# Rotating 96 images by 90 degrees: the first 2 MB loaded as 16 and 112 partitions in place of two halves

## The chip, the cores and the metric

The kernel runs on one core of one Trainium2 chip. The metric is the device time of one execution in microseconds (us); a run is given by its median over several executions. The traces come from the hardware profiler, one profiled execution each.

## The reference

The input `x` is an array of 32 x 3 x 256 x 256 float32 values, 25.17 MB. The reference turns each of the 96 images of 256 x 256 by 90 degrees; nothing is added or multiplied:

```python
def reference(x):
    return np.rot90(x, k=-1, axes=(-2, -1)).astype(np.float32)
```

So 25.17 MB are read from HBM, every element is moved to another place of its image, and 25.17 MB are written back.

## The kernel before

All of the input fits into SBUF at once, and the kernel rotates it there in place. The rows of all images lie behind each other (`rows_in`), and the work is cut into four groups of `sizes` = 2, 2, 4 and 4 slabs; a slab is 128 partitions times `E` = 4096 values (16 KB in each partition, 2 MB in all). Each group has its own tile `u` in `groups`, and no buffer is used for a second group, so that every load can be issued at the start.

SyncE (SP) issues all DMAs, loads and stores, on one queue, in the order of the program:

- Group 0, lines 65 to 69. Its two slabs are loaded one by one. `ld[s, i]` is half `i` of slab `s` in HBM: 128 pieces of 8 KB, one for each partition, 1 MB that lies together in HBM. `home[0]` and `home[1]` are the two slabs in SBUF, seen as (partition, half, 2048 values). `home[0]` is filled from `ld[1]` by two DMAs, one for each half (line 68), and `home[1]` from `ld[0]` by one DMA with both halves (line 69).
- Groups 1 to 3, lines 70 to 80. Group 1 comes in two DMAs to every second partition (64 of them, 16 KB pieces), groups 2 and 3 in four each to every fourth partition (32 of them, 32 KB pieces). The very last load is cut into a small part (line 77) and the rest (line 78).
- Stores, lines 191 to 211. Each group is stored in two halves, from the even and the odd partitions. The first store (line 195) has an added wait for the load of line 77 (`mark`); it is thereby kept behind nearly all loads. Most others go through `wide` (line 42). The last group's second half ends with two smaller stores (lines 208 and 209).

A DMA has a semaphore of its own while it is on its way. There are eight for them, used in turn, so the ninth load waits until the first has landed, the tenth until the second has, and so on.

VectorE does the transposing (`turn`, line 93), ScalarE copies (`copy`, line 96). Both run in the order written in the program; `keep` makes that order binding. The first work is `turn_slab(u[:, 0], spare)`: two transposes of half of slab 0 each, and either one reads both halves that line 68 loads. The second slab follows, then groups 1, 2 and 3, where a quarter block at a time is turned in place or parked in `spare`, `extra` or `most` until its place is free. A group's store waits for the last transpose or copy that touches it. TensorE does nothing, GpSimd only sets four constants at the start.

Of the kernel before, what the change touches and what calls it, by code (L numbers as in the profile page):

```python
# [9 lines left out]
def kernel(  # L10
# [14 lines left out]
    nc = tc.nc  # L25
# [3 lines left out]
    P = nc.NUM_PARTITIONS  # L29
# [31 lines left out]
    def rows_of(rows, n):  # L61
        return rows[first[n] * P * R : (first[n] + sizes[n]) * P * R]


    ld = rows_of(rows_in, 0).rearrange("(s i p r) w -> s i p (r w)", s=2, i=2, p=P)
    home = [groups[0][:, s].rearrange("p (i f) -> p i f", i=2) for s in range(2)]
    for i in range(2):
        nc.sync.dma_start(out=home[0][:, i], in_=ld[1, i])  # L68
    nc.sync.dma_start(out=home[1], in_=ld[0].transpose([1, 0, 2]))  # L69
    for n in range(1, len(sizes)):  # L70
        I = sizes[n]
        ld = rows_of(rows_in, n).rearrange("(a i m r) w -> i m a (r w)", a=2, i=I, m=P // I)
# [169 lines left out]
```

## Time and profile before

| what | value |
|---|---|
| median of 3 runs | 122.44 us (122.44 to 122.64) |
| the profiled execution | 122.47 us |
| its span, first to last instruction | 120.69 us |
| HBM read and written | 25.17 MB + 25.17 MB, 417 GB/s over the span |
| DMA packets | 2624, their time is 97.6% of 16 engines' span |
| VectorE busy | 83.3 us, 25 instructions |
| ScalarE busy | 40.0 us, 20 instructions |
| first load issued, first packet starts | 0.73, 1.75 us |
| the first two loads landed | 5.55 and 8.02 us |
| first transpose starts | 8.12 us |
| last load landed | 61.67 us |
| last store issued (issue ends), last packet ends, last store landed | 101.09, 119.49, 119.88 us |

Times within the execution count from the start of the span. A DMA is issued by SP in some 0.4 to 1.4 us (the issue is what the profile shows as SP's instruction); the data move later, in packets, on 16 DMA engines, and the DMA has landed when its semaphore has been raised by all of them. In the page's DMA row each digit is the share of busy time of the 16 DMA engines in one fortieth of the span, 3.02 us; the row below it gives the bytes moved. A line such as "SPq L195 <- DMA u<-in_x_dram: 29.8, 1, 29.8" says that SP's queue, at line 195, waited for a load: us in all, number of waits, longest wait.

### The profile page before, as it was taken

The numbers are of one execution on the slowest core, as the hardware profiler recorded it, in microseconds if no ns is written. First come the engines' busy times: TensorE is split into PE (matmuls) and PEld (weight loads), VectorE is DVE, ScalarE is ACT, GpSimd is POOL, SyncE is SP. The second block draws the span as 40 slices with busy tenths as digits, with TensorE's granted clock in tenths as the row PEclk, the third lists the DMA queues.
The fourth block names the chain that finished last, engine by engine and source line by source line (L and its number), as shares of the span: only waits on it lengthen the run. The fifth ranks groups of instructions, "written<-read, shape, count | busy, mean of one in ns | idle before, by whom it ended". The sixth has DMA issues, their size and how long they took to land.

```text
span 120.7 us, 135 instructions
## 1 busy us (share of the span) xinstructions
DVE 83.3 (69%) x25; ACT 40.0 (33%) x20; POOL 0.2 (0%) x4
## 2 busy tenths in 40 slices
DVE  0039999999995099999999999999999900000000
ACT  0000400380004199508459599709202800000000
POOL 0000000000000000000000000000000000000000
DMA  3999999998999999998989898989898989899694
GB/s 84 429 421 424 467 434 434 434 489 380 478 391 478 391 467 402 413 456 364 505 358 510 369 500 369 500 358 510 358 510 358 510 358 510 348 521 521 261 407 201
DMA packets 2624, 50.33 MB, mean 417 GB/s; under 512 B 384, under 2 KB 384, under 8 KB 448
## 3 DMA queue, kind: packets, MB, share of 16 engines
q1 hardware_dynamic: 2624, 50.33, 97.6%
HBM read 25.17 MB, written 25.17 MB: 417 GB/s over the span
## 4 chain that ended last, share of the span: by engine, by line
DVE 39%; DMA 28%; issue 4%; SPq 4%; ACT 3%; DVEq 0%
DVE u L93 32%; DMA u<-in_x_dram 28%; DVE extra L93 4%; ACT extra L96 3%; SPq L80 3%; DVE spare L93 2%; DVE most L93 2%; SPq L68 1%; SPq L69 0%; DVEq L93 0%
## 5 line engine op out<-in xcount | busy, mean ns | idle before, releaser
L93 DVE STREAM_TRANSPOSE u<-u 128x2048 f32<-128x2048 f32 x15 | 56.2, 3817 | 0.2
L93 DVE STREAM_TRANSPOSE spare<-u 128x2048 f32<-128x2048 f32 (+1 forms) x4 | 11.9, 3004 | 12.6 <-DMA u<-in_x_dram 12.6
L96 ACT COPY u<-spare 128x512 f32<-128x512 f32 (+2 forms) x8 | 10.0, 1288 | 15.1 <-DVE u L93 10.3
L96 ACT COPY u<-extra 128x1024 f32<-128x1024 f32 (+1 forms) x4 | 9.3, 2352 | 15.0 <-DVE u L93 11.1
L96 ACT COPY extra<-u 128x2048 f32<-128x2048 f32 x2 | 7.9, 3937 | 2.5 <-issue 2.5
L96 ACT COPY spare<-u 128x1024 f32<-128x1024 f32 (+1 forms) x3 | 5.7, 1897 | 3.1 <-DMA u<-in_x_dram 3.1
L96 ACT COPY u<-most 128x1792 f32<-128x1792 f32 x1 | 3.2, 3219 | 7.3 <-DVE u L93 7.3
L96 ACT ACT_TABLE_LOAD x1 | 1.3, 1283 | 13.1 <-DMA u<-in_x_dram 13.1
L93 DVE STREAM_TRANSPOSE extra<-extra 128x2048 f32<-128x2048 f32 x2 | 4.8, 2378 | 0.0
L93 DVE STREAM_TRANSPOSE extra<-u 128x2048 f32<-128x2048 f32 x1 | 3.9, 3898 | 0.0
L93 DVE STREAM_TRANSPOSE u<-spare 128x2048 f32<-128x2048 f32 x1 | 3.6, 3630 | 0.0
L96 ACT COPY most<-u 128x1792 f32<-128x1792 f32 x1 | 3.2, 3217 | 0.0
L93 DVE STREAM_TRANSPOSE spare<-spare 128x2048 f32<-128x2048 f32 x1 | 2.5, 2529 | 0.0
L93 DVE STREAM_TRANSPOSE most<-most 128x1792 f32<-128x1792 f32 x1 | 2.1, 2059 | 0.0
L226 POOL MEMSET const-bfloat16-1.0<- 128x1 bf16 x1 | 0.1, 102 | 0.0
L226 POOL MEMSET const-uint8-127<- 128x1 uint8 x1 | 0.1, 101 | 0.0
L226 POOL MEMSET const-float32-0.0<- 128x1 f32 x1 | 0.1, 99 | 0.2 <-issue 0.2
L226 POOL MEMSET const-float32-1.0<- 128x1 f32 x1 | 0.1, 98 | 0.0
## 6 DMA issues: line engine op xcount, KB each, us to landing
u<-in_x_dram SPq DMA_DIRECT2D x10, 2048.0 KB, 30.1
out_dram<-u SPq DMA_DIRECT2D x3, 4096.0 KB, 16.6
out_dram<-u SPq DMA_DIRECT2D x4, 2048.0 KB, 14.6
out_dram<-u SPq DMA_DIRECT2D x1, 3072.0 KB, 20.4
u<-in_x_dram SPq DMA_DIRECT2D x2, 1024.0 KB, 5.8
u<-in_x_dram SPq DMA_DIRECT2D x1, 1536.0 KB, 34.0
out_dram<-u SPq DMA_DIRECT2D x1, 768.0 KB, 20.9
u<-in_x_dram SPq DMA_DIRECT2D x1, 512.0 KB, 35.2
```

The costliest lines, as they stand in the source:

```text
L68: nc.sync.dma_start(out=home[0][:, i], in_=ld[1, i])
L80: nc.sync.dma_start(out=to[i::I], in_=ld[i])
L93: keep(nc.vector.transpose(out=out, in_=in_))
L96: keep(nc.scalar.copy(out=out, in_=in_))
L226: nc = _bacc.Bacc("TRN2", target_bir_lowering=False, num_devices=1)
```

## The change

The two DMAs of line 68 move the same 2 MB as before, in another division. Before, each took one half (8 KB) of all 128 partitions, 1 MB. Now the first takes both halves of partitions 0 to 15 (256 KB in 32 pieces of 8 KB), and the second both halves of partitions 16 to 127 (1.75 MB in 224 pieces). The place of every byte in HBM and SBUF, the number of DMAs, their order in the queue and all other code stay the same; the lines behind move down by one.

```diff
     home = [groups[0][:, s].rearrange("p (i f) -> p i f", i=2) for s in range(2)]
-    for i in range(2):
-        nc.sync.dma_start(out=home[0][:, i], in_=ld[1, i])
+    lead = 16
+    for p in (slice(0, lead), slice(lead, P)):
+        nc.sync.dma_start(out=home[0][p], in_=ld[1][:, p].transpose([1, 0, 2]))
     nc.sync.dma_start(out=home[1], in_=ld[0].transpose([1, 0, 2]))
```

## The prediction

> **What bounds the kernel now.** I read the page's DMA rows first, then the waits of SP's queue and of the engines, then the chain of waits, and last fine windows and the records of single packets over the first microseconds.
>
> ```profile
> DVE 83.3 (69%) x25; ACT 40.0 (33%) x20; POOL 0.2 (0%) x4
> ...
> DMA  3999999998999999998989898989898989899694
> GB/s 84 429 421 424 467 434 434 434 489 380 478 391 478 391 467 402 413 456 364 505 358 510 369 500 369 500 358 510 358 510 358 510 358 510 348 521 521 261 407 201
> ...
> q1 hardware_dynamic: 2624, 50.33, 97.6%
> ```
>
> The only slice in which the DMA engines are not full, apart from the last few, is the first (a 3 against 9s). Everything goes through one queue, and its packets fill 97.6% of the 16 engines' span. The records of single packets show the same from below: from the first packet at 1.75 us to the last at 119.49 the packets follow each other within some 10 ns on every engine. An 8 KB packet takes 0.309 us, nearly always; a 32 KB one 1.214. Adding up all packets at these median times gives 1,873 us, or 117.1 us for each of the 16 engines. First start 1.75 plus 117.1 is 118.85; the last packet really ends at 119.49. So all that is lost between is 0.64 us, and it is lost at the beginning:
>
> ```profile
> 1.60:1.80 0.20, 0.00 (x0) 0.00 (x0) 0.00 (x0) 1.00 1.27 205
> 1.80:2.00 0.20, 0.00 (x0) 0.00 (x0) 0.00 (x0) 1.00 0.88 164
> 2.00:2.20 0.20, 0.00 (x0) 0.00 (x0) 0.00 (x0) 1.00 1.62 205
> 2.20:2.40 0.20, 0.00 (x0) 0.00 (x0) 0.00 (x0) 1.00 0.45 82
> 2.40:2.60 0.20, 0.00 (x0) 0.00 (x0) 0.00 (x0) 1.00 0.49 164
> 2.60:2.80 0.20, 0.00 (x0) 0.00 (x0) 0.00 (x0) 1.00 0.00 0
> 2.80:3.00 0.20, 0.00 (x0) 0.00 (x0) 0.00 (x0) 1.00 1.00 410
> ...
> 3.20:3.40 0.20, 0.00 (x0) 0.00 (x0) 0.00 (x0) 1.00 1.16 492
> ```
>
> (Columns: window, sum, busy time of DVE, ACT, POOL, clock, DMA share, GB/s, each packet counted where it starts.) Until 2.8 us little moves: no packet starts between 2.6 and 2.8, and none ends between 2.24 and 2.85. The packet records tell two things apart. First, the starts are spread: eight engines start from 1.75 to 1.83, some 12 ns apart, four from 2.00 to 2.07, four from 2.48 to 2.52. Second, the first packets are slow wherever they started early: 0.95 to 1.13 us in place of 0.309 on eight engines. All engines run at full pace only from 2.86 to 3.20. The engines that started last (2.48 to 2.52) are not the ones behind: their first packets end at 2.88 to 2.89. Furthest behind are three that started at 2.02 to 2.07 and end their first packet at 3.03 to 3.06, so their second at 3.37.
>
> ```profile
> SPq L195 <- DMA u<-in_x_dram: 29.8, 1, 29.8
> SPq L42 <- DVE u L93: 27.3, 2, 20.2
> ...
> DVE spare L93 <- DMA u<-in_x_dram: 12.6, 2, 8.1
> ```
>
> VectorE's waits for loads (12.6 us in two) are what it has in hand: 8.1 before its first transpose and 4.5 before 42.29. SP's waits for VectorE (27.3) are spent with stores queued ahead: the last group's first store is issued at 96.35, when the last store of group 2 still runs to 100.49 (its landing). The stores' bytes are therefore also never late. So the bound is the slowest DMA engine from first packet to last, and a delay or gain of one engine at the start stays to the end, because it is given the same bytes afterwards.
>
> **What the change does, part by part.** Sum against the profiled execution, 122.47 us (median of the runs 122.44; span 120.69, so 1.78 lie outside it). A difference of 0.2%, 0.25 us, is about what a measurement of this kernel can tell from no change.
>
> *Issues.* Two DMAs of 128 partitions go, two of 16 and 112 come. Issue times of the three first loads:
>
> ```profile
> 0.73 0.40 SPq L68
> ...
> 1.19 0.42 SPq L68
> ...
> 1.65 0.43 SPq L69
> ```
>
> L69 has both halves, as the new ones do, and takes 0.43. So SP's queue moves by at most 0.04 us. The loads behind lie tens of microseconds in the queue before they land (30.1 us median), which hides it; without that cover it costs 0.04. The ninth load waits for the first transfer's landing (5.55) and the tenth for the second's (8.02); the first now comes sooner. VectorE still needs both transfers: it starts with the second's landing. A delay of up to 4.5 us there is covered by its idle time before 42.29, where it then waits for a load that has moved by as much.
>
> *Start of the engines.* First packet 1.02 us after the issue begins, as now. [...] With 32 packets in place of 128 all engines could start by about 1.85. Bounds: nothing gained, if the slow first packets end at 2.86 to 3.06 whenever they began (the engines that began late were not behind); 0.64 gained if the whole loss at the start goes. I take 0.1 by the former, since the row shows starts and ends unrelated; it stands inside the next term.
>
> *Between the two.* Two packets per engine last 0.62 us, to 2.37 at the earliest; the second transfer's packets come from 1.19 + 1.02 = 2.21, for the last engine, by the spread of 0.77 now, at 2.98. Cost 0 to 0.6; I take 0, as the term that follows lasts longer.
>
> *A narrow destination.* In the kernel before, all loads spread their partitions over the whole width, 128, every second or every fourth, and all run at 0.309 us per 8 KB. The lead sends 16 engines into 16 neighbouring partitions, which no row shows. Lower bound: engines don't disturb each other, 2 x 0.309 = 0.62. Upper bound: eight partitions are one engine's share now, so 16 are the share of two, and if the writes share the paths of two engines, 32 / 2 x 0.309 = 4.94. The groups of four in the start times are the nearest row: 16 partitions are then four groups, four engines to each, 8 packets behind each other: 8 x 0.309 = 2.47. I take that. From a start at 1.85 the lead ends at 4.32 on all engines, against 3.37 for the latest one now: +0.95. The present stall lies within these 2.47, as writes wait then anyway; if it adds, it is 0.64 more.
>
> [...]
>
> *112 partitions.* 14 packets per engine, seven partitions in place of eight, so an engine's share no longer begins where its share of other loads does. Bounds: 0, and, if two engines stand in each other's way half the time, 7 x 0.309 = 2.2. I take one packet for the slowest engine, 0.31, nearer the lower end as all strided loads of the trace run without loss.
>
> [...]
>
> *Sum:* 122.47 + 0.95 + 0.31 = 123.73, say 123.7.
>
> **The rivals.**
>
> *The early start counts (faster).* Neighbouring partitions cost nothing, all engines start by 1.85, and the slowest has two packets done by about 2.9 in place of 3.37: -0.45, 122.0; at most -0.64, 121.8. For it: the spread of the starts is real, and nothing in the trace shows one engine's write disturbing another's. Against: late starters weren't behind. It decides if the lead takes under some 1.2 us. Chance 0.26.
>
> *The stall decides (no change).* Whatever holds all packets from 2.24 to 2.85 holds the new ones too; the three latest engines gain 0.1 and lose it between the transfers: 122.4. Chance 0.11.
>
> *The 112 partitions collide (much slower).* The lead as in the forecast, and the misplaced shares cost the full 2.2: 122.47 + 0.95 + 2.2 = 125.6, with the stall on top 126.2. For it: lockstep engines at 0.309 us a packet would meet again and again. Against: the strided loads also spread otherwise and lose nothing. Chance 0.17.
>
> *The change doesn't spread the lead.* If partitions belong to engines by their place, 16 of them go to four engines, eight packets each, and the rest begin only with the second transfer, at 2.2 to 3.0. Each engine keeps its bytes; the latest ends its first packet some 0.3 later than 3.06: 122.8. Chance 0.07.
>
> **How the numbers follow.** Forecast 123.7, chance 0.39, its own range 122.9 (lead shared by few) to 124.8 (stall added, a second packet lost). Faster by over 0.2%: the first rival, 0.26. Within: the second, 0.11. Slower: 0.39 + 0.17 + 0.07 = 0.63. The range takes in 122.0 with what lies just below it, and reaches to just under 125.6; outside it remain the best of the first rival and most of the third, about 0.18. So 121.9 to 125.5.
>
> **What would show it.** If I am right, the first 2 packets of each engine take over 1 us each until some 4.3 us, the windows from 2.8 to 4.2 us show far under 400 GB/s, VectorE's first transpose moves from 8.12 to about 9.4, and the DMA tail moves by the same. If the first rival holds, the window 2.6 to 2.8 is full and the first transpose starts before 8. If the third, packets of 8 KB above 0.4 us appear all the way from 4.3 to 10 us. Wrong altogether would be a change at the end that the start of the DMA doesn't show: a gap among the stores, or VectorE late at 96.

## The result, and the profile after

The changed kernel takes 126.0 us (125.82 to 126.11 in 4 runs) against 122.5 for the one before: 1.0282 times as long, 95% interval 1.0265 to 1.03. Forecast were 123.7, with a range of 121.9 to 125.5. The direction was right, the size was not; the time is that of the third rival, the colliding 112 partitions (125.6, with the stall 126.2). The profiled execution took 125.82, 3.35 more than the one before.

First the fine windows of the changed kernel, in the columns of the prediction (window, sum, DVE, ACT, POOL, clock, DMA share, GB/s):

```profile
1.60:1.80 0.20, 0.00 (x0) 0.00 (x0) 0.00 (x0) 1.00 1.04 246
1.80:2.00 0.20, 0.00 (x0) 0.00 (x0) 0.00 (x0) 1.00 2.07 410
...
3.40:4.40 1.00, 0.00 (x0) 0.00 (x0) 0.00 (x0) 1.00 0.53 131
4.40:10.60 6.20, 0.00 (x0) 0.00 (x0) 0.00 (x0) 1.00 1.00 277
12.00:36.00 24.00, 23.90 (x7) 4.92 (x3) 0.00 (x0) 1.00 1.01 432
```

and the same stretches of the kernel before:

```profile
3.40:4.40 1.00, 0.00 (x0) 0.00 (x0) 0.00 (x0) 1.00 0.95 401
4.40:7.60 3.20, 0.00 (x0) 0.00 (x0) 0.00 (x0) 1.00 1.04 435
12.00:36.00 24.00, 23.86 (x7) 4.92 (x3) 0.00 (x0) 1.00 1.03 442
```

The lead does what it was cut for: by the packet records all 16 engines start between 1.73 and 1.92 us, where they were spread from 1.75 to 2.52. It does not help. From 3.4 to 4.4 the engines move 131 GB/s in place of 401, and then 277 in place of 435 for all the rest of the first slab. A DMA share of 1.00 beside 277 GB/s says that the engines are not short of work: every packet only lasts longer. From 4.4 to 10.5 us an 8 KB packet takes 0.473 us in the mean, against 0.310 before. From 12 to 36 us the rate is nearly what it was (432 against 442 GB/s; the second slab's own delay lies in this window).

VectorE follows, and its cover holds as forecast. It starts 3.56 us later, and what it then waits for is again a load:

```profile
11.68 7.08 DVE L94 STREAM_TRANSPOSE spare<-u 128x2048 f32<-128x2048 f32 x2 [11.68 <-DMA u<-in_x_dram]
```

```profile
DVE spare L94 <- DMA u<-in_x_dram: 16.2, 2, 11.7
```

Of 16.2 us of waiting 4.5 are still the second wait, as before; both ends moved together. The page of the changed kernel shows the loss in one place only, the second to fourth slices of the GB/s row (211, 296 and 333; before 429, 421 and 424):

```profile
GB/s 106 211 296 333 433 444 433 428 507 359 486 359 507 338 507 433 412 486 359 423 412 428 428 507 380 465 465 380 486 359 507 338 507 423 423 486 497 285 428 164
...
q1 hardware_dynamic: 2624, 50.33, 97.8%
```

The 97.8% is a warning: packets fill the engines as fully as before (97.6%), with 3.3 us more to the span. In this number a packet of 0.473 us and one of 0.310 look the same.

The loss can be laid out from the ends of the packets, by the time at which so much had been moved (MB of 1,048,576 bytes), and from the landings:

| moved | before | after | later by |
|---|---|---|---|
| 0.25 MB (after: the lead) | 3.34 | 3.37 | 0.03 |
| 0.375 MB | 3.64 | 4.38 | 0.74 |
| 2 MB (the first slab) | 7.64 | 10.57 | 2.93 |
| 4 MB (the second slab) | 12.55 | 15.92 | 3.37 |
| last packet | 119.49 | 122.80 | 3.31 |
| first slab landed | 8.02 | 11.58 | 3.56 |
| second slab landed | 12.99 | 16.48 | 3.49 |
| last store landed | 119.88 | 123.22 | 3.34 |

By the packets it is 0.74 up to the first packet behind the lead, 2.19 in the 13 packets per engine that follow (6.19 us in place of 4.00), 0.44 in the second slab, nothing after it. By the landings the second slab loses nothing (4.90 us behind the first, before 4.97): all of the loss is there when the first slab has landed. The loss at the start is nearly all still there at the end.

The packet records deceive where the packets are slow. The lead's packets are recorded as ended by 3.37 us, but its semaphore only rises from 4.46 to 4.79, 1.4 to 1.9 us later; in the kernel before the first transfer's last packet records and landings are some 0.34 us apart. The list of DMA issues (times issued, KB, us from issue to landing) has it:

```profile
u<-in_x_dram SPq DMA_DIRECT2D x1, 1792.0 KB, 10.4
...
u<-in_x_dram SPq DMA_DIRECT2D x1, 256.0 KB, 4.1
```

256 KB need 4.1 us to land. Less the 0.34, the lead ends at 4.12 to 4.45 (an estimate). The transfer behind it does the same on a smaller scale: its last packet is recorded as ended at 10.63, and it has landed at 11.58, 0.95 us later; in the kernel before it is 0.36. So the 0.44 that the packets show in the second slab were by the landings lost in the first. From the lead's landing to this one are 6.79 us, where 14 packets of 0.309 take 4.33: 2.46 lost.

### The profile page after: what moved, and what is told of

Its sections match the earlier page's. It is cut to its first block, busy times and chain, and to the rows that moved or that the text cites. A ratio compares the mean times of both kernels' runs of the same rounds, so it can differ in the third digit from the quotient of the medians.

```text
span 124.0 us, 135 instructions
## 1 busy us (share of the span) xinstructions
DVE 83.3 (67%) x25; ACT 40.1 (32%) x20; POOL 0.2 (0%) x4
## 3 DMA queue, kind: packets, MB, share of 16 engines
q1 hardware_dynamic: 2624, 50.33, 97.8%
## 4 chain that ended last, share of the span: by engine, by line
DVE 42%; DMA 32%; SPq 4%; issue 2%; DVEq 0%
DMA u<-in_x_dram 32%; DVE u L94 31%; DVE spare L94 6%; DVE extra L94 4%; SPq L81 3%; DVE most L94 2%; SPq L69 1%; SPq L70 0%; DVEq L94 0%
## 5 line engine op out<-in xcount | busy, mean ns | idle before, releaser
L94 DVE STREAM_TRANSPOSE spare<-u 128x2048 f32<-128x2048 f32 (+1 forms) x4 | 11.9, 2994 | 16.2 <-DMA u<-in_x_dram 16.2
```

The lines of the kernel that those rows point to most:

```text
L94: keep(nc.vector.transpose(out=out, in_=in_))
```

## The experiments

All are compared with the kernel before, with the runs of their own session (122.5 to 122.6).

**Is it the start, or the division?** e1_slab1 leaves the first slab alone and divides the second, whose packets have nothing to do with the cold start.

```diff
-    nc.sync.dma_start(out=home[1], in_=ld[0].transpose([1, 0, 2]))
+    for p in (slice(0, 16), slice(16, P)):
+        nc.sync.dma_start(out=home[1][p], in_=ld[0][:, p].transpose([1, 0, 2]))
```

> Line 68 is as before (two halves over 128 partitions); the 16 + 112 division is put on the second slab instead, whose packets all run at 0.309 us in the kernel before, far from the start. If the loss comes from the 112 partitions' shares (engines meeting in the writes, wherever it stands), packets of 8 KB between 7.5 and 13 us grow from 0.309 to 0.45 to 0.5 us, the second slab takes about 7 in place of 4.9 us, and the kernel is 2 to 3 us slower than before: 124.5 to 125.5. If the loss needs the cold start, the time stays at 122.4 to 122.7. If 16 neighbouring partitions are narrow, the first 32 packets of the slab take longer than 0.62 us: 1.2 to 2.5.

Measured: 126.92 us, 1.0363 (1.0344 to 1.0382), 4.4 us slower and so more than expected. The windows:

```profile
5.00:7.00 2.00, 0.00 (x0) 0.00 (x0) 0.00 (x0) 1.00 1.03 434
7.60:9.40 1.80, 0.00 (x0) 0.00 (x0) 0.00 (x0) 1.00 1.17 137
9.40:10.40 1.00, 0.96 (x1) 0.00 (x0) 0.00 (x0) 1.00 0.69 156
10.40:16.00 5.60, 5.60 (x2) 0.00 (x0) 0.00 (x0) 1.00 1.03 279
```

At full pace until 7 us, then the same picture as in the changed kernel: 137 GB/s in the lead, a second slow stretch where the 112 begin, 279 GB/s in the rest. The cold start isn't needed. Here the lead costs more, which fits the stall of the start hiding part of it in the changed kernel: by the packets 0.25 MB take from 7.55 to 9.44, 1.89 us in place of 0.61, and the 0.25 MB behind it 1.31. Up to the first packet behind the lead, as in the table above, it is 2.77 in place of 0.92 us: 1.85 lost, against 0.74 in the changed kernel.

**Are half-size transfers bad, or neighbouring partitions?** e2_even_odd and e3_low_high cut the first slab into 64 and 64, once strided, once neighbouring.

```diff
-    for i in range(2):
-        nc.sync.dma_start(out=home[0][:, i], in_=ld[1, i])
+    for p in (slice(0, P, 2), slice(1, P, 2)):      # e3_low_high: slice(0, 64), slice(64, P)
+        nc.sync.dma_start(out=home[0][p], in_=ld[1][:, p].transpose([1, 0, 2]))
```

> The first slab comes as the 64 even and then the 64 odd partitions, both halves of each, 1 MB per transfer. If what counts is whether a transfer's partitions are spread over the whole width in equal shares, this runs like the kernel before: 122.3 to 122.7, 8 KB packets at 0.309 us after the start. If any transfer under 128 partitions with both halves at the start loses, it lands above 124.

> The first slab comes as partitions 0 to 63 and then 64 to 127, both halves, 1 MB per transfer, four neighbouring partitions for each of 16 engines. If writes go through paths that belong to partitions, either transfer has half of the paths: packets of 0.5 to 0.62 us, 1 MB in about 5 in place of 2.5 us, and the kernel 3 to 5 us slower: 125.5 to 127.5. If only shares that don't divide the width evenly (7 of 112) hurt, 122.3 to 122.8.

Measured: even and odd 123.06 us, 1.0043 (1.0031 to 1.0056); low and high 127.45, 1.0403 (1.0389 to 1.0417). The same bytes, numbers of packets and transfers; from 4 to 12 us the first moves 426 GB/s, the second 211:

```profile
4.00:12.00 8.00, 3.29 (x1) 0.00 (x0) 0.00 (x0) 1.00 1.01 426
```

```profile
4.00:12.00 8.00, 0.00 (x0) 0.00 (x0) 0.00 (x0) 1.00 1.02 211
```

An 8 KB packet takes 0.309 us with partitions spread over all 128, and 0.64 with 64 neighbouring ones. That even and odd still lose 0.55 us is something else: the first issue takes 0.74 in place of 0.40 us, and the first packet starts at 2.25 in place of 1.75. Low and high start as late (2.27), so the 4.4 us between the two don't come from the start.

**SBUF or HBM?** Low and high also read HBM in other pieces than even and odd. Two kernels cross them: the SBUF side of one with the HBM side of the other.

```diff
-    for i in range(2):
-        nc.sync.dma_start(out=home[0][:, i], in_=ld[1, i])
+    for p, q in ((slice(0, 64), slice(0, P, 2)), (slice(64, P), slice(1, P, 2))):   # e10_even_from_low: p and q change places
+        nc.sync.dma_start(out=home[0][p], in_=ld[1][:, q].transpose([1, 0, 2]))
```

> SBUF partitions 0 to 63 and then 64 to 127 as in e3_low_high, but each is read from the HBM pieces that e2_even_odd reads (every second 8 KB piece), so the output has rows of the first group in other places. If the SBUF side makes e3_low_high slow, this is as slow: 127.0 to 127.9, packets of 0.64 us. If the HBM side does, it is as e2_even_odd: 122.9 to 123.2.

> The converse: even and then odd SBUF partitions as in e2_even_odd, read from the HBM pieces that e3_low_high reads (64 neighbouring ones), so the output has rows of the first group in other places. If the SBUF side decides, 122.9 to 123.2 and packets of 0.309 us; if the HBM side, 127.0 to 127.9 and 0.64 us.

Measured: e9_low_from_even 127.8 us, 1.0423 (1.0407 to 1.0439), 209 GB/s from 4 to 12 us; e10_even_from_low 123.12, 1.0036 (1.0022 to 1.0049), 422 GB/s:

```profile
4.00:12.00 8.00, 0.00 (x0) 0.00 (x0) 0.00 (x0) 1.00 1.00 209
```

```profile
4.00:12.00 8.00, 3.31 (x1) 0.00 (x0) 0.00 (x0) 1.00 1.01 422
```

The time goes with the SBUF partitions, not with the HBM pieces. This settles the side for 64 and 64; for 16 and 112 it is concluded from that, not tested.

**How does the loss go with the width?** e11_four32 and e13_eight16 bring the second slab in four transfers of 32 and in eight of 16 neighbouring partitions.

```diff
-    nc.sync.dma_start(out=home[1], in_=ld[0].transpose([1, 0, 2]))
+    for k in range(8):                                # e11_four32: range(4), 32 * k, 32
+        p = slice(16 * k, 16 * k + 16)
+        nc.sync.dma_start(out=home[1][p], in_=ld[0][:, p].transpose([1, 0, 2]))
```

> The first slab as before; the second slab, far from the cold start, comes in four transfers of 32 neighbouring partitions each, two per engine. If a path belongs to a block of eight neighbouring partitions, 32 of them have four paths: packets of 4 x 0.309 = 1.24 us, the slab takes 19.8 in place of 4.9 us, and the kernel some 15 us longer: 137. [...]

> The first slab as before, the second in eight transfers of 16 neighbouring partitions, one per engine, two packets each, far from the start. With four engines to a path: 1.24 us a packet, 19.8 us for the slab in place of 4.9, the kernel at 136 to 138. With two engines to a path: 0.62 us, 127 to 128. If 16 neighbouring partitions are not narrow, 122.5 to 123.

Measured in one run each: 127.83 and 134.81 us. In windows well inside the slab, four of 32 and then eight of 16:

```profile
12.00:15.00 3.00, 3.00 (x2) 0.00 (x0) 0.00 (x0) 1.00 1.02 218
```

```profile
9.00:22.00 13.00, 7.08 (x2) 0.00 (x0) 0.00 (x0) 1.00 1.02 128
```

32 partitions are as fast as 64 (218 and 208 GB/s in two windows of 3 us, against 211 in e3_low_high; packets of 0.64 us in both). Blocks of eight neighbours as a path, which would have given 137 us, are out. 16 partitions are slower again, 128 GB/s and 1.03 us a packet, though not by the factor of four that was put in the expectation (1.24 us); the eight transfers land some 2.06 us apart. Why it is 1.03 and not 1.24 wasn't tried.

**Only the 16?** e5_32_96 takes 32 partitions ahead and 96 behind, six per engine.

```diff
-    for i in range(2):
-        nc.sync.dma_start(out=home[0][:, i], in_=ld[1, i])
+    for p in (slice(0, 32), slice(32, P)):
+        nc.sync.dma_start(out=home[0][p], in_=ld[1][:, p].transpose([1, 0, 2]))
```

> The lead is 32 partitions and the rest 96, six per engine in place of seven. If the paths of neighbouring partitions decide, the loss is like that of 16 and 112: 125 to 127. If the odd number seven decides (an uneven place in groups of four), six loses clearly less: 123 to 124.5. If the start alone decides, 122.4 to 123.

Measured: 126.44 us, 1.0323 (1.0307 to 1.0339). By the packets the lead is quicker (0.5 MB moved at 4.19 us, in the changed kernel at 4.82), the 96 slower (packets of 0.57 to 0.61 us). A wider lead doesn't mend it, and it isn't the odd number seven alone.

**Which of the two transfers costs?** e12_rest_first only exchanges them; its edit is shown against the changed kernel.

```diff
-    for p in (slice(0, lead), slice(lead, P)):
+    for p in (slice(16, P), slice(0, 16)):
```

> The same two transfers in the other order: 112 partitions first, the 16 behind them. If the 112 lose by themselves, their packets take 0.45 to 0.5 us from the start, and 1.75 MB are there at about 9.3 us as in the changed kernel (9.6). If the lead in front upset them, they run at 0.309 and 1.75 MB are there at 7.1. The 16 partitions then no longer stand in the cold start: with four engines to a path they cost up to 8 x 0.309 = 2.47 us in place of 0.62, and the kernel is slower than the changed one, 126.5 to 127.8; if the narrow lead costs nothing anywhere, 125.7 to 126.2.

Measured: 126.64 us, 1.0329 (1.0315 to 1.0343). In two windows, the 112 and then the 16:

```profile
3.40:8.60 5.20, 0.00 (x0) 0.00 (x0) 0.00 (x0) 1.00 1.05 314
8.60:10.50 1.90, 0.00 (x0) 0.00 (x0) 0.00 (x0) 1.00 1.10 134
```

The 112 lose with nothing in front of them: by the packets 1.75 MB are there at 8.59 us, before at 7.03, so they lose at least 1.56 (packets can end before they land). The expected 9.3 was too late. Their packets lose a little less than behind the lead: from 0.375 to 1.75 MB they take 4.71 us, in the changed kernel 5.22, before 3.39. The 16 then take 1.89 us in place of 0.61, the same as in e1_slab1. Both transfers cost. By the packets the slab is there at 10.5 us in either order; it has landed at 12.33, in the changed kernel at 11.58, and the kernel is 0.6 us slower than that one.

**Can the early start be had without it?** e7_quarter makes the lead wide, e4_one leaves a single transfer for the first slab, in which the later engines would, as its author estimated, start up to 0.4 us later.

```diff
-    for i in range(2):
-        nc.sync.dma_start(out=home[0][:, i], in_=ld[1, i])
+    for p in (slice(0, P, 4), slice(2, P, 4), slice(1, P, 2)):          # e7_quarter
+        nc.sync.dma_start(out=home[0][p], in_=ld[1][:, p].transpose([1, 0, 2]))
... or, in place of these two lines,
+    nc.sync.dma_start(out=home[0], in_=ld[1].transpose([1, 0, 2]))      # e4_one
```

> The lead made small but wide: partitions 0, 4, 8 to 124 (32 of them, both halves), then 2, 6, 10 to 126, then the 64 odd ones. If the narrow width was all that was wrong with a small lead, packets run at 0.309 us and the engines start together: 121.9 to 122.4. If strided 32 or 64 partitions make the issue long, as the 0.74 us of e2_even_odd's first issue against 0.40 suggest, the first packet starts at 2.1 to 2.3 us and the time is 122.6 to 123.1.

> The first slab in one transfer of 128 partitions, both halves, 256 packets. If the spread of the engines' starts counted, the later engines, which would begin up to 0.4 us later with twice the packets handed out ahead of them, carry that to the end: 122.8 to 122.9. If what holds all engines until 2.8 us decides and the starts don't, 122.3 to 122.6, no change.

Measured: e7_quarter 124.22 us, 1.0128 (1.0111 to 1.0146), slower than both of its expectations. Its first issue takes 0.74 us and the first packet starts at 2.27, 0.5 later than before; most of the rest is lost from 4 to 7 us (303 GB/s, where even and odd have 415), with one packet of 1.76 us and a DMA share of 0.81, so some engines also stood without a packet. So transfers can be spread over the whole width and still lose; why these three do is open. e4_one 122.86, 1.0022 (1.0013 to 1.0031): half of its engines start at 2.43 to 2.48, 0.25 MB are moved at 3.65 in place of 3.34, and about 0.27 us stay to the end. This fits late starts that count a little, but its very first packet is late as well (1.82 in place of 1.75), and nothing separates the two. No version was faster than the kernel before.

## Why the prediction was wrong, point by point

- *The bound* was right: a delay of the DMA engines at the start (3.56 us when the first slab has landed) stands at the end (3.34 at the last landing), and VectorE and the stores cover nothing of it and add nothing.
- *The issues* cost nothing, as said: 0.37 and 0.41 us.
- *Start of the engines:* a start of all by 1.85 was the author's estimate; they start from 1.73 to 1.92. So the starts drew together to 0.19 us, as forecast, and nothing came of it, as the latest packets were not those of the late starters. Taken alone the point holds only roughly: e4_one, with later starts, lost 0.27. That the first packets are slow "wherever they started early" is too broad: of the twelve engines that start by 2.07, eight have slow ones, four take 0.34 to 0.41 us.
- *A narrow destination:* put at 0.95, with the lead at its end at 4.32 on all engines. By the packets it is 0.74; by the landings the lead is at its end at 4.12 to 4.45, at most 1.08 later than 3.37. This term, the boldest of the sum, was right in kind (the 16 neighbours ran at 137 GB/s in e1_slab1 and 134 in e12_rest_first) and nearly in size. No run shows its four engines to a path: the transfers of e13_eight16 land 2.06 us apart, where four engines to a path would give 2.47, and nothing ties the four to the groups of four in the start times, from which it was taken. That the present stall lies within the term fits e1_slab1, where the same lead away from the start costs 1.85.
- *112 partitions:* this step failed. It was put at 0.31, "nearer the lower end as all strided loads of the trace run without loss". Measured are 2.46 by the landings (2.19 by the packets, for the 13 behind the first); the upper bound of this very term was 2.2. The reason for the choice was no evidence: the strided loads cover the whole width in equal shares, which is just what 112 neighbouring partitions don't do. e2_even_odd against e3_low_high shows that 64 spread partitions run at 426 GB/s where 64 neighbours run at 211, and e12_rest_first that the 112 lose with nothing ahead of them, at least 1.56. It is not enough to be spread, though: e7_quarter lost 1.6 us too.
- *The sum* was 0.95 + 0.31 = 1.26; measured by the landings 1.08 + 2.46 = 3.54, of which 3.34 are left at the end. With the term at its upper bound, it is the third rival's 125.6, near the measured 125.82. Its reason, two engines in each other's way half of the time, is not shown. That rival had 0.17 and the forecast 0.39, with the same assumption in both, engines that share a path, which no trace shows as such. Having taken it for the lead, it should have been taken for the 112.
- *The first rival* (neighbouring partitions cost nothing) is refuted by e3_low_high and e9_low_from_even (127.45 and 127.8 us). *The second* (nothing changes) is refuted by the 3.5 us. *The fourth* (the lead on four engines) is refuted by the start of 16 engines within 0.19 us.
- *What would show it:* the packets above 0.4 us from 4.3 to 10 us are there, as listed for the third rival. The forecast's own sign, the lead's packets over 1 us each until 4.3, didn't come as written: they are recorded with 0.34 to 0.85 us, and it is the first packets behind them that take 1.02 to 1.20. The first transpose moved to 11.68, not to 9.4.

Not shown is which engine writes which partitions, in any of these transfers, and so why the 112 lose 0.16 us a packet, the 96 of e5_32_96 0.27 and the 64 of e3_low_high 0.33. It also wasn't separated why the packets of the 112 take a little longer behind the lead than with nothing ahead of them (0.47 against 0.44 us).

## What to carry to other kernels

Cut a load into SBUF along the bytes of a partition, or into even and odd partitions, but don't cut off neighbouring ones, and measure any other cut (e7_quarter lost 1.6 us with every fourth partition ahead): here even and odd partitions ran at 426 GB/s, 64 neighbours ran at 211 GB/s, 16 at about 130, and what was left behind the cut at 277, where whole transfers had 435. When a cost is bounded from both sides and a neighbouring term already rests on the same assumption, take the value that this assumption gives for both. And read the rate beside the DMA share: 1.00 with 277 GB/s was a queue whose 8 KB packets took 0.473 us in place of 0.310.

## What the runs showed of the hardware that was not expected

- Packets can be recorded as ended long before they have landed: the lead's records end by 3.37 us, its semaphore is full at 4.79. Where packets are slow, compare landings.
- The issue of a transfer of 64 partitions, or of 32 strided ones, with two pieces each takes 0.74 to 0.76 us as the first of the kernel, that of 128, 112, 32 or 16 neighbouring ones 0.37 to 0.43. The first packet then starts 0.5 us later. The kernel with even and odd partitions is 0.55 us slower, although its packets run at 0.309 us after the start.
- After a slab with slow packets the next slab of 128 partitions runs at 0.314 to 0.315 us a packet in place of 0.309; for its 16 packets per engine that is under 0.1 us. The 4 MB behind it are moved in 9.79 us, before in 9.77.
